# Two value projections as one group of 512 columns, and an earlier broadcast, in a two-layer encoder trunk

## The chip, the cores and the metric

The kernel runs on one core of one Trainium2 chip. The metric is the device time of one launch, in microseconds (us); smaller is better. Five engines work side by side on their own instruction streams: PE (TensorE, matmuls), DVE (VectorE), ACT (ScalarE), POOL (GpSimd) and SP (SyncE, which issues the loads). They meet at semaphores.

## The reference

Two layers, each with four token mixers that read the same normalised input, then gates, an output projection and a gated MLP. Two groups of 256 tokens share all weights; the kernel treats them as 512 tokens. Cut to what matters:

```python
for l in range(DEPTH):                       # DEPTH = 2
    h = rmsnorm(x, attn_norm[l])             # D_MODEL = 1024
    proj = h @ w_in[l]
    a_cols, b_cols, c_cols, d_cols, g_cols = jnp.split(proj, [p1, p2, p3, p4], axis=-1)
    o_a = diff_mixer(a_cols, ...)            # "a": differential attention, values 256 columns
    o_b = natten_mixer(b_cols, b_rpb[l])     # "b": neighbourhood attention with a bias, values 256 columns
    o_c = mla_mixer(c_cols, ...)             # "c": low-rank attention
    o_d = gqa_mixer(d_cols, ...)             # "d": grouped-query attention
    gates = jax.nn.sigmoid(g_cols)
    merged = sum(gates[i] * (o_i @ w_branch[l, i]) for i in range(4))
    x = x + merged @ w_out[l]
    x = x + conv_ffn(rmsnorm(x, ffn_norm[l]), ...)
return rmsnorm(x, final_norm)
```

## The kernel before, in words

**Arithmetic.** Every projection is a product of fp32 data split in two fp32r parts, high and low, and takes three matmuls: high by high, high by low, low by high (`mm3`, L302 to L305; for values L475 to L477). The activations are held as `xh` and `xl`, eight blocks of 128 channels by 512 tokens.

**Pieces.** The weights come as a list of pieces, in a fixed order (`_piece_order`, L133 to L154); a piece is at most 128 partitions by 1280 columns, the ones spoken of here are 128x1024. One piece makes one unit of the main loop (L1241 to L1271). `split_piece` (L284 to L300) makes the high half `wh` of a piece on ACT (L294) and the low half `wl` as a difference, the first half of its columns on DVE (L297) and the rest on POOL (L299). It is called two units ahead (LOOK = 2), and there are three buffers each for raw, high and low pieces, so a piece's high half waits until the matmuls that read the piece three before have ended.

**Order at the start of a layer.** Units are bq0 bk0 bq1 bk1 (queries and keys of the neighbourhood mixer, whose pieces hold two channel blocks of all four, in four PSUM banks), aq0 ak0 (differential mixer), vb0 vb1 (neighbourhood values), aq1 ak1, vd0 vd1 ve0 ve1 vf0 vf1 (the other two mixers), va0 va1 (differential values), then the gates g0 to g31. A value group has two pieces with four channel blocks each. Its first unit issues no matmul, the second issues all 96 with 256 columns: four token tiles, each in a bank of its own over all eight blocks, each copied out by ACT as it ends (`v_unit`, L462 to L479; `v_evac`, L481 to L484).

**Around the change.** The normalisation factor per token, `rs`, is first broadcast to a row by four transposes on PE (`rb`, L364) into the one bank of pool pso; DVE copies it to `rsrow` (`norm_row`, L387 to L403, the copy in L393), and POOL makes `cosr` and `sinr` from it (L400, L401). In layer 0 these transposes are a hook inside aq0, after the third channel block (L602). ak0 uses the same bank of pso. `b_evac` (L636 to L645) scales a bank by `rsrow` on DVE (`bc`, L641), and `split` makes the high half on ACT (L308) and the low half on DVE (L309): bq0h, bq0l, bk0h, bk0l and so on. Scores (`scores_rows`, L784) go to two banks of pool psx; the biased copy `sb` (L795) frees such a bank, then DVE takes the maximum (L801), ACT the exponentials (L807), DVE scales (L817) and PE transposes (L827). `pair_gen` (L851 to L894) spreads these steps over units; PLAG says how many units lie ahead of the product with the values (`po`, L882), CPOS after which gate the first low-rank piece stands. The small `lam` operations (L1232, L1234) are made once. On each engine instructions run in the order in which the program issues them.

Of the kernel before, what the change touches and what calls it, by code (L numbers as in the profile page):

```python
# [32 lines left out]
GX = [(25, 29), (31, 32)]  # L33
GBR = {n: n - BLAG for n in range(BLAG, 30)} | {30: 29, 31: 30}
TLAG = {"a": 1, "b": 1, "c": 0, "d": 0}
PLAG = {"a": 2, "b": 0, "c": 1, "d": 2}
GAP = {"a": 3, "b": 2, "c": 2, "d": 3}
START = {"a": ("ak0", 9), "b": ("bk0", 4), "c": ("cv", 6), "d": ("vf1", 2)}
SLAB = ["bq0", "bk0", "bq1", "bk1"]
CLAG = 1  # L40
CPOS = 7
NEG = -1e30

G_ATTN, G_FFN = 0, 8
# [17 lines left out]
def _col_blocks():  # L62
    r = lambda a, n: list(range(a, a + n))
    blocks = []
    blocks.append(("va", r(A0 + 512, 256)))
    blocks.append(("vb", r(B0 + 512, 256)))
    blocks.append(("vd", r(D0 + 384, 128) + r(D0 + 256, 128)))
    dq = [c for g in range(2) for n in range(2) for c in r(D0 + 128 * n + 64 * g, 64)]
    blocks.append(("ve", r(C0 + 320, 32) + dq))
    blocks.append(("vf", r(C0 + 192, 128) + r(C0, 192)))  # L70
    for j in range(2):
        blocks.append((f"aq{j}", r(A0 + 128 * j, 128)))
        blocks.append((f"ak{j}", r(A0 + 256 + 128 * j, 128)))
    for j in range(2):
        blocks.append((f"bq{j}", r(B0 + 128 * j, 128)))
        blocks.append((f"bk{j}", r(B0 + 256 + 128 * j, 128)))
    return blocks


def _layout_weights(w_in, c_w_uq, c_w_ukv, w_branch, w_out, w_ffn_in, w_ffn_out):  # L80
# [5 lines left out]
    for l in range(DEPTH):  # L86
        p, slab = {}, {}
        for nm, cols in _col_blocks():
            a = kt(w_in[l][:, cols])
            if nm[0] == "v":  # L90
                p[nm + "0"] = a[:, 0:4]
                p[nm + "1"] = a[:, 4:8]
            elif nm in SLAB:
                slab[nm] = a
            else:
                p[nm] = a
        for q, nm in enumerate(SLAB):
            p[nm] = np.stack([slab[b][:, k] for k in (2 * q, 2 * q + 1) for b in SLAB], axis=1)
        z = np.zeros((128, 2, 384), np.float32)
        z[:, 0] = c_w_uq[l][0:128]  # L100
        z[0:64, 1] = c_w_uq[l][128:192]
        p["cq"] = z
        ukv = c_w_ukv[l].reshape(128, 4, 128)
        p["ck"] = ukv[:, :, 0:64]
        p["cv"] = ukv[:, :, 64:128]
        br = []
        for i, d in GSEQ:
            wb = w_branch[l, i]
            if i == 3:
                wb = wb.reshape(2, 2, 64, DM).transpose(1, 0, 2, 3).reshape(256, DM)  # L110
            br.append(kt(wb[:, d * 128:d * 128 + 128]))
        for n, (i, d) in enumerate(GSEQ):
            g = kt(w_in[l][:, G0 + i * DM + d * 128:G0 + i * DM + d * 128 + 128])
            p[f"g{n}"] = np.concatenate([g, br[GBR[n]]], axis=1) if n in GBR else g
        for q, (a, b) in enumerate(GX):
            p[f"gx{q}"] = np.concatenate(br[a:b], axis=1)
        for d in range(ND):
            p[f"wo{d}"] = kt(w_out[l][:, d * 128:d * 128 + 128])
        for j in range(NF):
            p[f"fu{j}"] = kt(w_ffn_in[l][:, j * 128:j * 128 + 128])  # L120
            p[f"fg{j}"] = kt(w_ffn_in[l][:, 2816 + j * 128:2816 + j * 128 + 128])
        fo = kt(w_ffn_out[l])
        for d in range(ND):
            a = fo[:, :, d * 128:d * 128 + 128]
            p[f"fo{d}_0"] = a[:, 0:8]
            p[f"fo{d}_1"] = a[:, 8:15]
            p[f"fo{d}_2"] = a[:, 15:22]
        for nm, a in p.items():
            pieces[(l, nm)] = a
# [3 lines left out]
def _piece_order():  # L133
# [1 line left out]
    two_ = [m for m in ORD if m in "ab"]  # L135
    qk = [[f"{m}q0", f"{m}k0", f"{m}q1", f"{m}k1"] for m in two_]
    assert qk[0] == SLAB
    names += qk[0] + qk[1][:2] + [f"v{two_[0]}0", f"v{two_[0]}1"]
    rest = {"x": qk[1][2:], "w": [f"v{two_[1]}0", f"v{two_[1]}1"], "d": ["vd0", "vd1", "ve0", "ve1"], "c": ["vf0", "vf1"]}
    for ch in 'xdcw':  # L140
        names += rest[ch]
    for n in range(32):
# [65 lines left out]
def trunk_kernel(ctx: ExitStack, tc: tile.TileContext, xt, wflat, gains, lams, rpb, consts, yt):  # L208
# [75 lines left out]
    def split_piece(i, parts=1, only=None):  # L284
# [7 lines left out]
        for q in range(parts):  # L292
            a, b = q * w, q * w + w
            S.activation(out=wh[:, a:b], in_=raw[:, a:b], func=AF.Copy)  # L294
            c = b if only is V else (a + b) // 2
            if c > a:
                V.tensor_tensor(out=wl[:, a:c], in0=raw[:, a:c], in1=f(wh[:, a:c]), op=ALU.subtract)  # L297
            if b > c:
# [26 lines left out]
    st = {}  # L325
# [130 lines left out]
    def build_layer(l):  # L456
# [21 lines left out]
                    evac(t, o)  # L478
            return pe0, pe1  # L479

        def v_evac(vt):  # L481
            def evac(t, o):
                S.activation(out=vt[:, t], in_=o, func=AF.Copy, scale=st["rs"][:, t:t + 1])
            return evac  # L484

        def row_tables():
            def go():
# [105 lines left out]
        def lin(nm, m=128, pool=pm):  # L593
            def pe(wh, wl):
# [4 lines left out]
                w = [a[:, :8 * m].rearrange("p (k c) -> p k c", k=8) for a in (wh, wl)]  # L599
                for k in range(8):  # L600
                    mm3(ps[:m], w[0][:, k], w[1][:, k], st["xh"][k], st["xl"][k], k == 0, k == 7)
                    if k == 2 and pool is pst and "row" in hooks:  # L602
                        hooks.pop("row")()
            return pe

# [494 lines left out]
        specs = {}  # L1100
        for nm in ("aq0", "ak0", "aq1", "ak1"):
            specs[nm] = (lin(nm, pool={"aq0": pst, "ak0": pso}.get(nm, pm)), a_evac(nm))
        for nm, n, ev in (("va", 256, v_evac(vA)), ("vb", 256, v_evac(vB)), ("vd", 256, vd_evac), ("ve", 288, ve_evac),
                          ("vf", 320, vf_evac)):
            pe0, pe1 = v_unit(nm, n, ev)
            specs[nm + "0"], specs[nm + "1"] = (pe0, None), (pe1, None)
# [134 lines left out]
    for i, u in enumerate(units):  # L1241
# [19 lines left out]
        for _, e in now:  # L1261
            e()
        vec(1)
        split_piece(i + LOOK, *((2, V) if i + LOOK < 4 else ()))
        load_piece(i + LOOK + RAW_BUFS)
        if u["now"] and u["evac"] is not None:
            u["evac"]()
# [60 lines left out]
```

## Time and profile before

| what | value |
|---|---|
| median of 3 runs | 1630.31 us (1630.29 to 1631.59) |
| profiled execution: its time | 1630.35 us |
| its span | 1628.6 us |
| PE busy | 1610.0 us, 99% |
| DVE, ACT, POOL busy | 59%, 38%, 40% |
| DMA | 149.26 MB, mean 92 GB/s |

Busy time of PE is from the start of a matmul to its modelled end, and pipelined matmuls overlap; their true pace is the distance between starts. A number in brackets at the end of a row is idle time ahead of the instruction on its engine, with the instruction that released it. "x2" marks instructions in a row that the view has put into one line.

### The profile page before, as it was taken

How to read it: one execution, taken by the hardware profiler on the slowest of the kernel's cores; microseconds unless marked ns; L12 is line 12 of the kernel's file. 1: busy time of each engine (PE TensorE's matmuls, PEld its weight loads, DVE VectorE, ACT ScalarE, POOL GpSimd, SP SyncE). 2: the span in 40 equal slices, each digit the busy share in tenths (PEclk: the TensorE clock that was granted, in tenths of full speed). 3: DMA queues.
4: the chain of work that ended last, by engine and by line, in shares of the span. 5: the costliest groups of instructions: out<-in, count | busy, mean ns of one | idle time of the engine just before them, and what ended most of it. 6: DMA issues, size and time to landing. Idle time of an engine off the chain costs nothing.

```text
span 1628.6 us, 21341 instructions
## 1 busy us (share of the span) xinstructions
PE 1610.0 (99%) x8163; PEld 1336.9 (82%) x8163; DVE 962.7 (59%) x1581; ACT 622.7 (38%) x1112; POOL 653.0 (40%) x443
## 2 busy tenths in 40 slices
PE   9999999999999999999999999999999999999997
PEld 7898788888888888888878977888788888888886
DVE  6767485656775666633366666755468656665113
ACT  4446454332333333322224555434332333333221
POOL 2432223435534444434444231244455344444342
PEclk9999999999999999999999999999999999999998
DMA  7212122221322222232232222222222222222331
GB/s 240 81 53 98 55 98 81 81 78 62 113 91 91 104 104 91 88 105 96 102 115 73 68 89 70 82 87 76 81 78 103 93 97 95 104 91 91 101 97 63
DMA packets 51016, 149.26 MB, mean 92 GB/s; under 512 B 13281, under 2 KB 16353, under 8 KB 50913
## 3 DMA queue, kind: packets, MB, share of 16 engines
q1 hardware_dynamic: 49824, 146.84, 26.5%
q8 instruction: 64, 1.05, 0.2%
q10 hardware_dynamic: 1088, 1.05, 0.2%
q14 instruction: 40, 0.32, 0.1%
HBM read 145.77 MB, written 2.10 MB: 91 GB/s over the span
## 4 chain that ended last, share of the span: by engine, by line
PE 97%; DVE 1%; issue 1%; ACT 1%; POOL 0%; POOLq 0%; DVEq 0%; ACTq 0%
PE pf L303 10%; PE pf L305 10%; PE pf L304 10%; PE pg L303 7%; PE pg L304 7%; PE pg L305 7%; PE pfo L303 5%; PE pfo L305 5%; PE pfo L304 5%; PE po L882 2%; PE pt L827 2%; PE pb L305 2%; PE pwo L304 2%; PE pwo L303 2%; PE pb L303 2%; PE pb L304 2%
## 5 line engine op out<-in xcount | busy, mean ns | idle before, releaser
L299 POOL TENSOR_TENSOR wl<-raw,wh 128x512 fp32r<-128x512 f32 (+4 forms) x258 | 447.3, 1735 | 570.7 <-ACT wh L294 455.3
L294 ACT ACTIVATE wh<-raw 128x1024 fp32r<-128x1024 f32 (+5 forms) x266 | 282.1, 1061 | 437.7 <-PE pfo L304 132.3
L297 DVE TENSOR_TENSOR wl<-raw,wh 128x512 fp32r<-128x512 f32 (+4 forms) x266 | 259.8, 977 | 230.6 <-ACT wh L294 219.2
L303 PE MATMUL pf<-xh,wh 128*128 128x512 f32 x704 | 274.3, 390 | 0.0
L305 PE MATMUL pf<-xh,wl 128*128 128x512 f32 x704 | 274.0, 389 | 0.0
L304 PE MATMUL pf<-xl,wh 128*128 128x512 f32 x704 | 274.0, 389 | 0.0
L303 PE MATMUL pg<-xh,wh 128*128 128x512 f32 x512 | 203.5, 397 | 0.4
L304 PE MATMUL pg<-xl,wh 128*128 128x512 f32 x512 | 199.9, 390 | 0.0
L305 PE MATMUL pg<-xh,wl 128*128 128x512 f32 x512 | 199.6, 390 | 0.0
L305 PEld LDWEIGHTS pf<-xh,wl 128*128 128x128 f32 x704 | 132.1, 188 | 27.7
L304 PEld LDWEIGHTS pf<-xl,wh 128*128 128x128 f32 x704 | 132.2, 188 | 27.3
L303 PEld LDWEIGHTS pf<-xh,wh 128*128 128x128 f32 x704 | 132.2, 188 | 27.1
L303 PE MATMUL pfo<-ah,wh 128*128 128x512 f32 (+1 forms) x374 | 141.1, 377 | 0.0
L304 PE MATMUL pfo<-al,wh 128*128 128x512 f32 (+1 forms) x374 | 140.8, 377 | 0.0
L305 PE MATMUL pfo<-ah,wl 128*128 128x512 f32 (+1 forms) x374 | 140.8, 377 | 0.0
L951 POOL TENSOR_TENSOR mg<-mg,gz 128x512 f32<-128x512 f32 x48 | 64.4, 1346 | 165.5 <-DVE gz L950 165.5
L309 POOL TENSOR_TENSOR al<-fc,ah 128x512 fp32r<-128x512 f32 x44 | 57.8, 1313 | 178.9 <-ACT ah L308 178.9
L303 PEld LDWEIGHTS pg<-xh,wh 128*128 128x128 f32 x512 | 96.2, 188 | 23.4 <-DVE gz L971 1.5
L305 PEld LDWEIGHTS pg<-xh,wl 128*128 128x128 f32 x512 | 96.1, 188 | 20.7
L304 PEld LDWEIGHTS pg<-xl,wh 128*128 128x128 f32 x512 | 96.3, 188 | 18.2
L972 ACT ACTIVATE gz<-gz 128x512 f32<-128x512 f32 x64 | 40.3, 630 | 133.9 <-DVE gz L971 133.8
L807 ACT ACTIVATE pr<-sc,mx 128x256 f32<-128x256 f32 x128 | 59.0, 471 | 73.5 <-DVE mx L802 73.5
(388 smaller groups left out, 2844.6 us busy)
## 6 DMA issues: line engine op xcount, KB each, us to landing
raw<-in_w_dram SPq DMA_DIRECT2D x156, 512.0 KB, 3.2
raw<-in_w_dram SPq DMA_DIRECT2D x58, 640.0 KB, 3.8
raw<-in_w_dram SPq DMA_DIRECT2D x32, 448.0 KB, 3.1
raw<-in_w_dram SPq DMA_DIRECT2D x4, 576.0 KB, 3.4
xall<-in_xt_dram SPq DMA_DIRECT2D x8, 256.0 KB, 5.2
raw<-in_w_dram SPq DMA_DIRECT2D x8, 256.0 KB, 5.3
bias<-in_rpb_dram SPq DMA_DIRECT2D x32, 64.0 KB, 3.3
out_dram<-y SPq DMA_DIRECT2D x4, 256.0 KB, 2.4
```

The source lines that it names most:

```text
L294: S.activation(out=wh[:, a:b], in_=raw[:, a:b], func=AF.Copy)
L297: V.tensor_tensor(out=wl[:, a:c], in0=raw[:, a:c], in1=f(wh[:, a:c]), op=ALU.subtract)
L299: G.tensor_tensor(out=wl[:, c:b], in0=raw[:, c:b], in1=f(wh[:, c:b]), op=ALU.subtract)
L303: PE.matmul(ps, lhsT=wh, rhs=xh, start=first, stop=False)
L304: PE.matmul(ps, lhsT=wh, rhs=xl, start=False, stop=False)
L305: PE.matmul(ps, lhsT=wl, rhs=xh, start=False, stop=last)
L309: (eng or V).tensor_tensor(out=l, in0=v, in1=f(h), op=ALU.subtract)
L807: S.activation(out=p[:, qt * 256:qt * 256 + 256], in_=src[c][:, qt * 256:qt * 256 + 256], func=AF.Exp, scale=sc, bias=mx[:, i:i + 1], accu ...
L827: PE.transpose(out=ps[:, kt * 256 + qt * 128:kt * 256 + qt * 128 + 128], in_=p[:, qt * 256 + kt * 128:qt * 256 + kt * 128 + 128], identity ...
L882: PE.matmul(ops[64 * e:64 * e + 64, :256], lhsT=v_of(mix, j, e, 2 * b + kt), rhs=pt[:, kt * 256:kt * 256 + 256], start=(kt == 0), stop=(kt ...
L951: G.tensor_tensor(out=m, in0=m, in1=z, op=ALU.add)
L972: S.activation(out=z, in_=z, func=AF.Tanh, scale=0.5)
```

## The change

The two groups of 256 value columns become one group "vw" of 512 columns, neighbourhood first. Its four pieces hold two channel blocks each, and stand where vb0 and vb1 stood: vw0 to vw3, then aq1, ak1, vd, ve, vf, gates. All four token tiles are open at once, in four banks, and the channel blocks are the outer loop over the pieces; within the last piece the token tile is the outer loop, so that the banks end one after another. ACT makes its eight copies of 256 columns after vw3. The broadcast hook in aq0 comes after the first channel block. In layer 0 the low halves of pieces 6 and 7 (vw0 and vw1, before vb0 and vb1) are made by POOL alone, in one instruction each. PLAG of the neighbourhood mixer is 4, and CPOS is 9.

```diff
-PLAG = {"a": 2, "b": 0, "c": 1, "d": 2}
+PLAG = {"a": 2, "b": 4, "c": 1, "d": 2}
...
-CPOS = 7
+CPOS = 9
...
-    blocks.append(("va", r(A0 + 512, 256)))
-    blocks.append(("vb", r(B0 + 512, 256)))
+    blocks.append(("vw", r(B0 + 512, 256) + r(A0 + 512, 256)))
...
+            if nm == "vw":
+                for q in range(4):
+                    p[f"vw{q}"] = a[:, 2 * q:2 * q + 2]
...
-    names += qk[0] + qk[1][:2] + [f"v{two_[0]}0", f"v{two_[0]}1"]
-    rest = {"x": qk[1][2:], "w": [f"v{two_[1]}0", f"v{two_[1]}1"], "d": ["vd0", "vd1", "ve0", "ve1"], "c": ["vf0", "vf1"]}
+    names += qk[0] + qk[1][:2] + [f"vw{q}" for q in range(4)]
+    rest = {"x": qk[1][2:], "w": [], "d": ["vd0", "vd1", "ve0", "ve1"], "c": ["vf0", "vf1"]}
...
-            c = b if only is V else (a + b) // 2
+            c = b if only is V else a if only is G else (a + b) // 2
...
+        def vw_pe(q):
+            def pe(wh, wl):
+                if q == 0:
+                    D["vw"] = [psum("psvw") for _ in range(4)]
+                w = [a[:, :1024].rearrange("p (k c) -> p k c", k=2) for a in (wh, wl)]
+                kt = [(k, t) for k in range(2) for t in range(4)]
+                if q == 3:
+                    kt.sort(key=lambda i: i[1])
+                for k, t in kt:
+                    d = 2 * q + k
+                    xh = st["xh"][d][:, t * 128:t * 128 + 128]
+                    xl = st["xl"][d][:, t * 128:t * 128 + 128]
+                    o = D["vw"][t]
+                    PE.matmul(o, lhsT=xh, rhs=w[0][:, k], start=(d == 0), stop=False)
+                    PE.matmul(o, lhsT=xh, rhs=w[1][:, k], start=False, stop=False)
+                    PE.matmul(o, lhsT=xl, rhs=w[0][:, k], start=False, stop=(d == 7))
+            return pe
+
+        def vw_evac():
+            for t, o in enumerate(D.pop("vw")):
+                for vt, c in ((vB, 0), (vA, 256)):
+                    S.activation(out=vt[:, t], in_=o[:, c:c + 256], func=AF.Copy, scale=st["rs"][:, t:t + 1])
...
-                    if k == 2 and pool is pst and "row" in hooks:
+                    if k == 0 and pool is pst and "row" in hooks:
...
+        for q in range(4):
+            specs[f"vw{q}"] = (vw_pe(q), vw_evac if q == 3 else None)
...
-        split_piece(i + LOOK, *((2, V) if i + LOOK < 4 else ()))
+        split_piece(i + LOOK, *((2, V) if i + LOOK < 4 else (1, G) if i + LOOK in (6, 7) else ()))
```

DVE in layer 0, from the row factor on, before (`rs2` is its square, `wl6` and `wl7` are low halves of pieces 6 and 7, `lam` the lambda values):

```order
L397 TENSOR_TENSOR rs2_406<-rs_332 128x4
L297 TENSOR_TENSOR wl6_456<-raw6_265,wh6_455 128x512
L1232 TENSOR_TENSOR lam_85<-lp_346 128x1 x2
L1234 TENSOR_SCALAR lam_85<-lam_85 128x1 x2
L297 TENSOR_TENSOR wl7_524<-raw7_296,wh7_523 128x512
L393 COPY rsrow_404<-rb_399 128x512
L641 TENSOR_TENSOR bc_427<-psbq0_199,rsrow_404 128x8x64
L309 TENSOR_TENSOR bq0l_430<-bc_427,bq0h_429 128x512
```

The same place now:

```order
L399 TENSOR_TENSOR rs2_400<-rs_332 128x4
L1254 TENSOR_TENSOR lam_85<-lp_346 128x1 x2
L1256 TENSOR_SCALAR lam_85<-lam_85 128x1 x2
L395 COPY rsrow_398<-rb_393 128x512
L661 TENSOR_TENSOR bc_427<-psbq0_199,rsrow_398 128x8x64
L311 TENSOR_TENSOR bq0l_430<-bc_427,bq0h_429 128x512
```

The two low halves are gone from DVE, and the copy of the broadcast row follows the lambda values directly; POOL's instructions on wl6 and wl7 are 128x1024 in the same places of its own order.

DVE further on in layer 0, between the scalings of the first softmax and the biased copy of the second, before:

```order
L630 TENSOR_TENSOR rc_513<-rc_513,rsh_514 128x512
L810 RECIPROCAL ri_503<-su_502 128x2
L817 TENSOR_SCALAR sb_504<-sb_504,ri_503 128x256 x2
L309 TENSOR_TENSOR aq0l_520<-rc_513,aq0h_519 128x512
L795 SCALAR_TENSOR_TENSOR sb_533<-sc_463,bias1_374 128x512
```

The same place now:

```order
L650 TENSOR_TENSOR rc_512<-rc_512,rsh_513 128x512
L830 RECIPROCAL ri_502<-su_501 128x2
L837 TENSOR_SCALAR sb_503<-sb_503,ri_502 128x256 x2
L299 TENSOR_TENSOR wl9_641<-raw9_459,wh9_640 128x512
L311 TENSOR_TENSOR aq0l_519<-rc_512,aq0h_518 128x512
L815 SCALAR_TENSOR_TENSOR sb_559<-sc_462,bias1_374 128x512
```

A low half, that of piece 9, now stands ahead of the biased copy that frees the second score bank.

PE where the values of layer 0 meet the second pair of scores (`psvb` and `psvw` are banks of the values, `sc` of scores), before:

```order
L477 MATMUL psvb_573<-wh7_523,xl7_184 128x256
L475 MATMUL psvb_599<-wh6_455,xh0_123 128x256
L784 MATMUL sc_559<-bk0h_435,bq0h_429 128x256
L784 MATMUL sc_559<-bk0l_436,bq0h_429 128x256
L784 MATMUL sc_559<-bk0h_435,bq0l_430 128x256
```

The same place now:

```order
L496 MATMUL psvw_531<-wh6_455,xh1_140 128x512
L497 MATMUL psvw_531<-wl6_456,xh1_140 128x512
L498 MATMUL psvw_531<-wh6_455,xl1_141 128x512
L804 MATMUL sc_585<-bk0h_435,bq0h_429 128x256
L804 MATMUL sc_585<-bk0l_436,bq0h_429 128x256
```

The scores stood behind 25 matmuls of 256 columns, the last of them of the second token tile; now they stand behind the 24 of vw0, with 512 columns. The next six scores, of the other bank, stood 37 matmuls of 256 columns later, and stand 13 of 512 later now.

## Rows read from the trace of the kernel before

**Rows 1.** Page, parts 1 and 4: busy us by engine; the chain's shares by engine.
```profile
PE 1610.0 (99%) x8163; PEld 1336.9 (82%) x8163; DVE 962.7 (59%) x1581; ACT 622.7 (38%) x1112; POOL 653.0 (40%) x443
...
PE 97%; DVE 1%; issue 1%; ACT 1%; POOL 0%; POOLq 0%; DVEq 0%; ACTq 0%
```

**Rows 2.** Waits of PE: us in total, times, longest.
```profile
PE sc L784 <- DVE sb L795: 2.6, 3, 1.1
...
PE psak L303 <- DVE rsrow L393: 2.4, 1, 2.4
```

**Rows 3.** Timeline of PE, values: start, us, line, tile, shape; first and last of 95.
```profile
123.89 0.28 PE L476 MATMUL psva<-wl,xh 128*128 128x256 f32 x1
...
135.16 0.28 PE L477 MATMUL psva<-wh,xl 128*128 128x256 f32 x1
```

**Rows 4.** Timeline of PE, matmuls of 512 columns, first and last of 24.
```profile
19.84 0.39 PE L303 MATMUL psbq<-xh,wh 128*128 128x512 f32 x1
...
25.06 0.39 PE L305 MATMUL psbk<-xh,wl 128*128 128x512 f32 x1
```

**Rows 5.** Timeline of PE in layer 0, from aq0's last matmul to the values.
```profile
34.64 0.39 PE L305 MATMUL psaq<-xh,wl 128*128 128x512 f32 x1
37.41 0.47 PE L303 MATMUL psak<-xh,wh 128*128 128x512 f32 x1 [2.39 <-DVE rsrow L393]
...
42.60 0.39 PE L784 MATMUL sc<-bk0l,bq0h 64*128 64x256 f32 x2
...
44.66 0.28 PE L475 MATMUL psvb<-wh,xh 128*128 128x256 f32 x1
...
48.90 0.35 PE L784 MATMUL sc<-bk0h,bq0h 64*128 64x256 f32 x1 [1.10 <-DVE sb L795]
...
54.93 0.35 PE L784 MATMUL sc<-bk0h,bq0h 64*128 64x256 f32 x1 [0.58 <-DVE sb L795]
...
55.80 0.39 PE L476 MATMUL psvb<-wl,xh 128*128 128x256 f32 x1
```

**Rows 6.** Timeline of DVE in layer 0.
```profile
30.63 1.31 DVE L1232 TENSOR_TENSOR lam<-lp 128x1 f32<-128x1 f32 x2
...
35.97 0.69 DVE L297 TENSOR_TENSOR wl<-raw,wh 128x512 fp32r<-128x512 f32 x1 [3.85 <-ACT wh L294]
36.58 0.68 DVE L393 COPY rsrow<-rb 128x512 f32<-128x512 f32 x1
...
40.90 1.65 DVE L309 TENSOR_TENSOR bk0l<-bc,bk0h 128x512 fp32r<-128x512 f32 x1 [0.70 <-ACT bk0h L308]
...
46.38 1.78 DVE L309 TENSOR_TENSOR bk1l<-bc,bk1h 128x512 fp32r<-128x512 f32 x1
48.08 0.68 DVE L795 SCALAR_TENSOR_TENSOR sb<-sc,bias 128x512 f32<-128x512 f32 x1
...
54.10 0.68 DVE L795 SCALAR_TENSOR_TENSOR sb<-sc,bias 128x512 f32<-128x512 f32 x1
```

**Rows 7.** Timeline of ACT in layer 0: piece 7's high half, a copy of values.
```profile
34.88 1.06 ACT L294 ACTIVATE wh<-raw 128x1024 fp32r<-128x1024 f32 x1 [4.80 <-POOL bias L744]
...
47.73 0.47 ACT L483 ACTIVATE vB<-psvb,rs 128x256 f32<-128x256 f32 x1 [1.48 <-PE psvb L477]
```

**Rows 8.** Timeline of POOL in layer 0: piece 6's low half, sinr.
```profile
30.07 1.79 POOL L299 TENSOR_TENSOR wl<-raw,wh 128x512 fp32r<-128x512 f32 x1 [5.00 <-ACT wh L294]
...
39.01 1.75 POOL L401 TENSOR_TENSOR sinr<-rsrow,cst 128x512 f32<-128x512 f32 x1
```

**Rows 9.** Groups of POOL by form: busy us, mean ns of one, idle before.
```profile
L497 POOL TENSOR_TENSOR rt<-cst,lv 128x256 f32<-128x256 f32 x8 | 5.9, 737 | 0.0
...
L400 POOL TENSOR_TENSOR cosr<-rsrow,cst 128x512 f32<-128x512 f32 x2 | 2.6, 1293 | 0.0
```

**Rows 10.** Timelines of PE and DVE in layer 1, second score bank.
```profile
849.91 0.38 PE L784 MATMUL sc<-bk0h,bq0h 64*128 64x256 f32 x1 [0.92 <-DVE sb L795]
...
849.17 0.68 DVE L795 SCALAR_TENSOR_TENSOR sb<-sc,bias 128x512 f32<-128x512 f32 x1
```

More of the change, by code (lines that the diff above doesn't have):

```diff
@@ L89, in _layout_weights @@
             a = kt(w_in[l][:, cols])
-            if nm[0] == "v":
+            if nm == "vw":
+                for q in range(4):
+                    p[f"vw{q}"] = a[:, 2 * q:2 * q + 2]
+            elif nm[0] == "v":
                 p[nm + "0"] = a[:, 0:4]
@@ L479, in v_unit @@
             return pe0, pe1
[L481 to L484, printed above, removed]
+        def vw_pe(q):
[19 more added lines that the diff above has]
+                    S.activation(out=vt[:, t], in_=o[:, c:c + 256], func=AF.Copy, scale=st["rs"][:, t:t + 1])
         def row_tables():
@@ L1102, in build_layer @@
             specs[nm] = (lin(nm, pool={"aq0": pst, "ak0": pso}.get(nm, pm)), a_evac(nm))
-        for nm, n, ev in (("va", 256, v_evac(vA)), ("vb", 256, v_evac(vB)), ("vd", 256, vd_evac), ("ve", 288, ve_evac),
+        for q in range(4):
+            specs[f"vw{q}"] = (vw_pe(q), vw_evac if q == 3 else None)
+        for nm, n, ev in (("vd", 256, vd_evac), ("ve", 288, ve_evac),
                           ("vf", 320, vf_evac)):
```

## The prediction

> **What bounds the kernel now.** I read the page's busy shares and its chain first, then the table of TensorE's waits, then the timeline where those waits stand. TensorE is busy 99% of the span and is 97% of the chain [rows 1]. A change can therefore gain in two ways only: fewer or shorter matmuls, or the removal of one of the few places where TensorE stands still. Those places are known: it waits for the row factor's copy once, 2.4 us, and for a score bank three times, 2.6 us in all [rows 2]. The profiled execution took 1630.35 us, 0.04 above the median of 1630.31; my sum is made against 1630.35, of which the span is 1628.6. All of the span counts, since TensorE fills it to its end.
>
> **Packing.** Removed: 192 matmuls of 256 columns per layer (two groups of four token tiles, eight blocks, three terms). Added: 96 of 512 columns. With 256 columns, 95 matmuls in a row start between 123.89 and 135.16, 94 steps of 0.1199 us [rows 3]. With 512 columns, 24 in a row start between 19.84 and 25.06, 23 steps of 0.2270 [rows 4]. Two small ones cost 0.2398, one large one 0.2270: 0.0128 saved per pair, 96 pairs per layer, two layers: **2.46 us**. The Trainium skill ("TensorE: Matmul & The Clock Gate", Back-to-back issue gap) gives a matmul its columns at 2.4 GHz and 2.5 ns; by that the packing would save 192 × 2.5 ns = 0.5 us. The rows show five times that per matmul and decide, since both forms stand in this trace with the same operand type. Bounds: nothing (if the new matmuls run at 0.2398, as the order of their operands is new) and 2.5.
>
> **The hook, and the splits moved to POOL (layer 0 only).** Before, aq0's last matmul starts at 34.64, so ak0 could start near 34.87; it starts at 37.41 [rows 5], because ak0 takes the bank of the broadcast, and DVE copies that bank only at 36.58, behind the low split of piece 7, which waits for ACT's high half [rows 6, 7]. Now the broadcast stands six matmuls earlier (some 1.36 us, so near 29.6) and DVE has no split of pieces 6 and 7. What then blocks the copy is less: the two tiny lambda operations stood from 30.63 to 31.94 while POOL did its half of piece 6 [rows 6, 8]. That half becomes a whole: 128x256 takes 0.737 on POOL and 128x512 1.293 [rows 9], so 0.556 for 256 more, and 128x1024 is an estimate of 1.293 + 2 × 0.556 = 2.4. POOL starts at 30.07, so lambda runs at 32.45 and the copy ends near 33.3. ak0 follows aq0 without a wait: **2.54 us earlier**.
>
> Little of it is kept. ACT's order is unchanged: the high half of piece 7, held until aq0 gives its buffer back, runs from 34.88 to 35.94 [rows 7], and only then bq0's high half, to 36.5. POOL's low split of piece 7 starts then too and lasts to about 38.4. DVE's low half of bq0 needs two inputs from SBUF, as POOL does. Such DVE instructions take 0.69 alone and 1.65 or 1.78 beside a POOL instruction [rows 6], ending about 0.55 after it: they wait for it to finish. The rows show this for POOL instructions of 1.3 us, none for one of 2.4. The Trainium skill ("SBUF — State Buffer", Who interferes with whom) has the shared pair as a lock held for the whole instruction, which speaks against handing POOL whole splits; if it holds, bq0's low half ends at 38.9, if the pair is given up half way, near 37.2. I take the first, as the nearest rows do the same. Then follow bk0's copy (39.5), 0.7 for its high half (the idle time ahead of its low half in [rows 6], 40.2), and its low half, behind sinr, which POOL takes first (1.75 in [rows 8], 1.3 without a rival): it ends near 41.9. Before, it ended at 42.55 and the first scores that read it started at 42.60 [rows 5, 6]. So TensorE, 2.5 us ahead, waits some 2 us more there, and is **0.67 us ahead** when the values start: 43.99, not 44.66.
>
> Before, the second pair of scores comes one by one: the first after 25 small matmuls, where TensorE stands still about 1.25 us until 48.90, the second another 0.75 until 54.93 (by start steps; the idle times of the rows are 1.10 and 0.58) [rows 5]. Now they stand behind 24 and 37 large ones. TensorE reaches the first at 43.99 + 24 × 0.227 = 49.44, when DVE's biased copy for them, started at 48.08 before and 0.6 earlier now, is done: no wait. It reaches the second at 53.26. Their bank is freed by DVE's next biased copy, which was at 54.10 [rows 6]. That copy now has the split of piece 9 ahead of it, since vw0's buffer comes back after 24 matmuls and not after a whole group. Piece 9's high half runs to 52.15, POOL holds its low half to 53.45 (1.3), DVE's scalings (0.6), own half (0.69) and aq0's low half (0.69) follow it: the copy ends near 55.8, and **the wait is 2.5 instead of 0.75**. Were POOL no obstacle there, 1.9.
>
> Set side by side at the restart: before at 55.80 with 130 small matmuls left (15.6 us, ends 71.4); now, after six score matmuls, at 56.7 with 59 large ones left (13.4 us, ends 70.1). **Layer 0 gains 1.33 us**: 1.23 is packing, so the removed waits (2.54, 1.25, 0.75) come back as waits of about 2 and 2.5 almost in full.
>
> **Layer 1** has neither hook nor the POOL splits; there the order alone changes. Its second scores started at 849.91 after an idle 0.92 (1.14 by start steps), because the bank was freed by a copy from 849.17 on [rows 10]. They now stand behind vw0, 5.4 us later, and the wait goes: **1.14**, with 1.23 of packing. The split that now gets ahead of the next biased copy does not delay TensorE: that copy stands before it there.
>
> **What costs nothing.** Eight ACT copies of 256 columns per layer, as before, 0.47 each [rows 7], but now in one go after vw3. aq1 takes the first bank alone, which is complete 18 matmuls (4.1 us) before the group ends, while ACT needs 0.94 for its two copies and about as much for the exponentials between. Were that cover gone, each layer would wait up to all eight. Four banks for the group: the last needs bk1's scaled copy, at 44.5, and is first written at 46.0. vw0 and vw1 need POOL's whole splits by 44 and 49.5; they are done at 32.5 and 38.4. PLAG 4 puts neighbourhood's products later, when their values exist; CPOS 9 moves the low-rank projections two gates later, and the three score waits of [rows 2] all lie ahead of the gates [rows 5, 10]. Loads have the same sizes and count.
>
> **Sum:** 1.33 + 1.14 + 1.23 = 3.70 to take from 1630.35, **1626.65 us**. About 0.2% (3.26 us, so 1627.05 and below) is what a measurement of this kernel can tell from no change; the forecast is just past it.
>
> **Rivals.**
> *A, packing alone.* Each wait removed, layer 1's too, comes back elsewhere. For it: layer 0 does so by my working. Against it: no instruction stands newly ahead of layer 1's copy. 1630.35 − 2.46 = 1627.9, no measurable change.
> *B, the waits of layer 0 go for good.* If POOL does not hold DVE during the long splits (or they are shorter than 2.4), bq0's and bk0's low halves end near 37.2 and 39.3, TensorE hardly waits for the first scores, and the chain behind follows 2.5 us earlier: 2.54 + 0.15 + 1.25 + 0.75 = 4.7 saved, with 2.46 and 1.14 it is 8.3: 1622.0; half of it is 1624.5. For it: the chain bk0, biased copy, scaling is all that is late. Against it: 1.65 and 1.78 in [rows 6].
> *C, the packing doesn't pay.* The new matmuls load token tiles as weights and step at 0.2398, not 0.2270; then 2.46 falls away and 1629.1 is left, no change. Against it: weight loads are as large in [rows 4]. The skill's 2.5 ns, by itself, would leave 1628.6, in the same class.
> *D, slower.* One group holds all four banks, and its copies come at the end. If ACT is held by the exponentials between (they wait for DVE's maxima), and the first bank's two copies finish more than 4.1 us after its last matmul, aq1 waits, and ak1 after it; with all eight, 8 × 0.47 = 3.75 per layer, or 7.5 in two. 1626.65 + 7.5 = 1634.15. It decides between vw3's end and aq1's first matmul. For it: an exponential and a copy of transposes stand ahead of them in ACT's order, and both wait on other engines. Against it: what these wait for is done before vw3 begins.
>
> **Numbers.** Forecast 0.49 (its own range 1625.6 to 1627.6, by 1 us either way for the two waits of layer 0 that I worked out), A 0.20, B 0.17, C 0.06, D 0.08. Faster: B's 0.17 and some 0.39 of the forecast, 0.56. Same: A, C and the forecast's upper tenth, 0.36. Slower: D, 0.08. The range runs from half of B's gain past the forecast, 1623.8, to between A and C, 1628.6; D, the far half of B and part of C are left out, about 2 in 10.
>
> **What would show it.** Right: value matmuls at steps of 0.227; ak0 less than 0.3 after aq0; TensorE idle about 2 us at the first scores for bk0's low half; POOL's 128x1024 near 2.4 and DVE's bq0 low half near 2.4 beside it; no wait at the second scores in either layer; one of about 2.5 at the next, behind the split of piece 9. Wrong: an idle TensorE ahead of aq1 or ak1 (D), a step of 0.24 (C), DVE at 0.69 beside POOL's long split (B), or waits in the gates of either layer, where none is now.

## The result, and the profile after

The change makes the kernel slower: 1651.43 us (median of 4, 1649.76 to 1653.64) against 1630.9, a ratio of 1.0122 with a 95% interval of 1.0109 to 1.0134. The prediction was 1626.65, the range 1623.8 to 1628.6. The profiled execution took 1649.76 us, its span 1648.0, that is 19.4 us more than the span of before.

TensorE is hardly busier than before (1613.8 us against 1610.0), but the chain now lies 91% on it, where it was 97% [rows 1]. The rest is waits; first the chain's shares, then lines of the table of TensorE's waits of the changed kernel (us in total, times, longest):

```profile
PE 91%; DVE 4%; issue 2%; ACT 2%; POOL 0%; SPq 0%; DMA 0%; POOLq 0%; ACTq 0%; DVEq 0%
```

```profile
PE pg L305 <- DVE cql L311: 6.1, 2, 3.1
PE pg L305 <- DVE gz L991: 4.8, 2, 2.4
...
PE po L902 <- ACT ptr L853: 2.4, 2, 1.2
PE sc L804 <- DVE sb L815: 2.2, 1, 2.2
PE psve L477 <- DVE rtm L534: 1.5, 2, 0.8
...
PE sc L804 <- ACT bk0h L310: 1.4, 1, 1.4
PE cv L738 <- DVE cql L311: 1.4, 2, 0.7
...
PE sc L804 <- DVE bk0l L311: 0.6, 1, 0.6
```

Those that stand twice, once per layer, are all new and all lie behind the place that the prediction worked out: among the projections (psve), the gates (pg), and the low-rank pieces (cv). Before, TensorE had no wait there: beside the lines of [rows 2] its table has only waits at the ends of the kernel and at each layer's broadcast. The single ones are the layer-0 waits that were forecast.

**Layer 0, up to the values: as forecast.** TensorE's timeline of the changed kernel (start, us, line, tile, idle time ahead), answering to [rows 5]:

```profile
35.21 0.39 PE L305 MATMUL psak<-xh,wh 128*128 128x512 f32 x1
...
40.63 0.38 PE L804 MATMUL sc<-bk0h,bq0h 64*128 64x256 f32 x2 [1.41 <-ACT bk0h L310]
...
42.27 0.39 PE L804 MATMUL sc<-bk0l,bq0h 64*128 64x256 f32 x2 [0.60 <-DVE bk0l L311]
...
44.33 0.39 PE L496 MATMUL psvw<-wh,xh 128*128 128x512 f32 x1
...
49.86 0.38 PE L804 MATMUL sc<-bk0h,bq0h 64*128 64x256 f32 x1
...
56.23 0.35 PE L804 MATMUL sc<-bk0h,bq0h 64*128 64x256 f32 x1 [2.23 <-DVE sb L815]
```

ak0 follows aq0 without a wait, 2.0 us are then lost at the first scores, the second pair's first scores don't wait, its second wait 2.2. DVE and POOL (a timeline, and POOL's group of that form) show why:

```profile
30.46 2.44 DVE L1254 TENSOR_TENSOR lam<-lp 128x1 f32<-128x1 f32 x2 [0.87 <-ACT lp L1251]
...
33.00 0.68 DVE L395 COPY rsrow<-rb 128x512 f32<-128x512 f32 x1
...
36.84 2.47 DVE L311 TENSOR_TENSOR bq0l<-bc,bq0h 128x512 fp32r<-128x512 f32 x1 [2.44 <-ACT bq0h L310]
...
55.40 0.68 DVE L815 SCALAR_TENSOR_TENSOR sb<-sc,bias 128x512 f32<-128x512 f32 x1
```

```profile
L301 POOL TENSOR_TENSOR wl<-raw,wh 128x1024 fp32r<-128x1024 f32 x2 | 4.8, 2398 | 5.7 <-ACT wh L296 5.7
```

A low half that takes 0.69 us alone [rows 6] takes 2.47 beside POOL's instruction of 2.40.

**The gates: where the time went.** TensorE, DVE and POOL in layer 0 (the same in layer 1):

```profile
156.98 0.65 PE L902 MATMUL po<-ptr,vA 128*64 128x256 f32 x4 [1.20 <-ACT ptr L853]
160.04 0.50 PE L305 MATMUL pg<-xh,wh 128*128 128x512 f32 x1 [2.42 <-DVE gz L991]
...
241.39 0.48 PE L305 MATMUL pg<-xh,wh 128*128 128x512 f32 x1 [3.06 <-DVE cql L311]
```

```profile
149.89 1.97 DVE L579 TENSOR_TENSOR dr<-dr,r 128x384 f32<-128x384 f32 x4
151.77 1.28 DVE L821 TENSOR_REDUCE mx<-sc 128x2 f32<-128x512 f32 x2
...
156.64 2.15 DVE L839 SCALAR_TENSOR_TENSOR pr<-pr,ri 128x256 f32<-128x256 f32 x2
158.72 0.68 DVE L821 TENSOR_REDUCE mx<-sc 128x2 f32<-128x512 f32 x1
159.32 0.67 DVE L991 TENSOR_TENSOR gz<-pg,rsrow 128x512 f32<-128x512 f32 x1
...
236.93 1.53 DVE L321 TENSOR_TENSOR nt<-nt,nh 128x16 f32<-128x16 f32 x1
238.50 0.17 DVE L322 SCALAR_TENSOR_TENSOR ny<-nt,ny 128x16 f32<-128x16 f32 x1
238.71 0.76 DVE L669 COPY ex<-ny 128x512 f32<-128x512 f32 x2
...
240.57 0.68 DVE L311 TENSOR_TENSOR cql<-tq,cqh 96x512 fp32r<-96x512 f32 x1
```

```profile
236.24 2.19 POOL L301 TENSOR_TENSOR wl<-raw,wh 128x640 fp32r<-128x640 f32 x1 [3.87 <-ACT wh L296]
```

DVE in the same place of layer 0 before:

```profile
150.93 1.28 DVE L801 TENSOR_REDUCE mx<-sc 128x2 f32<-128x512 f32 x2
...
155.79 0.88 DVE L819 SCALAR_TENSOR_TENSOR pr<-pr,ri 128x256 f32<-128x256 f32 x2
```

At 160 the gate waits for a bank that DVE's `gz` frees, and DVE comes to it only after the differential pair's scalings, held by a split on POOL (2.15 us for two that took 0.88 in the same place before). That hold is 1.3 us. The rest began earlier: the pair's maxima start 4.4 us after its scores (151.77 after 147.37), 1.4 before the change (150.93 after 149.53); ahead of them on DVE now stand the late normalisation's steps, the four `dr` last. The exponentials follow the maxima, and behind them and a piece's high half on ACT stands the copy `ptr` (from 156.32), for which the products wait at 157.

At 241 the gate waits for `cql`. Ahead of that on DVE stand the last Newton steps (the iteration for the reciprocal square root) and copies of the differential mixer's normalisation, and one of these steps took 1.53 us instead of 0.17, beside POOL's half of the next piece. What a wait costs does not end with it. The windows of the changed kernel (length, TensorE busy, granted clock, DMA share, GB/s):

```profile
156.00:160.00 4.00, 0.65 (x4) 1.00 0.00 0
160.00:165.00 5.00, 4.96 (x15) 0.66 0.41 131
...
970.00:976.00 6.00, 5.71 (x18) 0.72 0.32 109
...
1050.00:1056.00 6.00, 4.45 (x13) 0.72 0.24 96
```

After TensorE stood nearly still from 156 to 160, the granted clock fell from 2.4 to 1.2 GHz for about 3 us (0.66 over 5 us; large matmuls start 0.43 apart instead of 0.227), which costs (1 − 0.66) × 5 = 1.7 us more. The other two windows give 0.28 × 6 = 1.7 each.

By start steps (the distance between two starts, less the step that the matmuls ahead had among themselves), the new waits are 0.93 (psve), 1.51 and 2.67 (157 and 160), 3.28 (241) and 0.87 (cv) per layer, 9.26, so 18.5 in two layers. With three slow stretches of 1.7 that is 23.6. Less the 3.70 that the prediction had as gain, 19.9 is left; the spans differ by 19.4. The idle times in the rows are 0.2 to 0.3 shorter each; with them it would be 17.6.

### The profile page after: what moved, and what is told of

Same layout as the page of the kernel before. It is cut to its first block, busy times and chain, and to the rows that moved or that the text cites. A ratio compares the mean times of both kernels' runs of the same rounds, so it can differ in the third digit from the quotient of the medians.

```text
span 1648.0 us, 20960 instructions
## 1 busy us (share of the span) xinstructions
PE 1613.8 (98%) x7971; PEld 1329.3 (81%) x7971; DVE 952.8 (58%) x1579; ACT 621.6 (38%) x1112; POOL 657.6 (40%) x443
## 4 chain that ended last, share of the span: by engine, by line
PE 91%; DVE 4%; issue 2%; ACT 2%; POOL 0%; SPq 0%; DMA 0%; POOLq 0%; ACTq 0%; DVEq 0%
PE pf L305 10%; PE pf L306 10%; PE pf L307 10%; PE pg L305 7%; PE pg L306 7%; PE pg L307 7%; PE pfo L305 5%; PE pfo L307 5%; PE pfo L306 5%; PE po L902 2%; PE pwo L306 2%; PE pwo L305 2%; PE pwo L307 2%; PE pb L306 2%; PE pb L305 2%; PE pb L307 2%
## 5 line engine op out<-in xcount | busy, mean ns | idle before, releaser
L301 POOL TENSOR_TENSOR wl<-raw,wh 128x512 fp32r<-128x512 f32 (+5 forms) x258 | 450.7, 1747 | 576.1 <-ACT wh L296 499.2
L299 DVE TENSOR_TENSOR wl<-raw,wh 128x512 fp32r<-128x512 f32 (+4 forms) x264 | 251.2, 951 | 239.4 <-ACT wh L296 227.1
L991 DVE TENSOR_TENSOR gz<-pg,rsrow 128x512 f32<-128x512 f32 x64 | 43.9, 686 | 70.5 <-PE pg L307 70.4
```

The costliest lines, as they stand in the source:

```text
L301: G.tensor_tensor(out=wl[:, c:b], in0=raw[:, c:b], in1=f(wh[:, c:b]), op=ALU.subtract)
L991: V.tensor_tensor(out=z, in0=pg, in1=st["row"], op=ALU.mult)
```

## The experiments

All times are medians; each ratio is to the kernel before, run beside it (1631.65 to 1631.93 us in these runs).

**What part of the change makes the loss.** Four kernels, each the kernel before with a part of it. The first has the new order of the pieces, with PLAG and CPOS as in the change, but two value groups of 256 columns.

```diff
-PLAG = {"a": 2, "b": 0, "c": 1, "d": 2}
+PLAG = {"a": 2, "b": 4, "c": 1, "d": 2}
...
-CPOS = 7
+CPOS = 9
...
-    for ch in 'xdcw':
+    for ch in 'wxdc':
```

> The kernel before with the order of the pieces changed alone: both value groups stay apart, of 256 columns each, but the differential values stand right behind the neighbourhood's, and the other two mixers' projections come two units later; PLAG of the neighbourhood mixer is 4 and CPOS 9 as in the change. No packing, hook and splits as before. Phase theory (the change's loss is that the normalisation of the other two mixers and the three low-rank pieces now fall into the same units as the softmax steps of the differential and grouped-query pairs): about 1650 us, with TensorE waits near 157, 160, 241 and 251 us as in the change. Packing theory (four banks held at once and k outermost make the loss): within 2 us of 1630. Layer-0 theory (hook and POOL splits delay all that follows): within 2 us of 1630.

Measured: 1659.26, ratio 1.0170 (1.0155 to 1.0185), with every one of the new waits: 0.91 before psve, 1.50 and 2.68 near 160, 3.28 and 0.87 near 244 and 255. So the order with CPOS, without packing, makes more than the whole loss.

```diff
-CPOS = 7
+CPOS = 9
```

> The kernel before with CPOS 9 instead of 7 alone: the low-rank pieces two gates later, everything else where it was. If the low-rank units alone cause the waits at 241 and 251 us (3.28 and 0.87 us, in both layers) it is some 8 us slower, about 1638; the waits at 157 and 160 are absent. If it takes both (normalisation late and pieces late), it is within 2 us of 1630.

Measured: 1647.84, ratio 1.0093 (1.0077 to 1.0110). The two waits are there at their size (3.28 and 0.87) and none near 157. They make 8.3 us; the forecast of 8 had left out the clock, which in the profiled execution was low in four stretches of 1.7 each:

```profile
36.00:42.00 6.00, 4.41 (x13) 0.72 0.59 204
...
236.00:242.00 6.00, 3.37 (x8) 0.72 0.32 111
...
858.00:864.00 6.00, 5.40 (x32) 0.72 0.27 87
...
1050.00:1056.00 6.00, 6.00 (x21) 0.72 0.00 0
```

The first and the third stand behind ak0's wait of 2.4 us and behind the 1.1 us wait of [rows 10], which this kernel has as the kernel before has them; in that one's profiled execution the clock stayed at 1.00 behind both.

```diff
-PLAG = {"a": 2, "b": 0, "c": 1, "d": 2}
+PLAG = {"a": 2, "b": 4, "c": 1, "d": 2}
```

> The kernel before with PLAG of the neighbourhood mixer 4 instead of 0 alone: its products with the values four units later. Phase theory: within 2 us of 1630, as these are 8 short matmuls per pair beside gates. Rival (the later products take the pso bank and ACT's copies when the differential pairs want them): slower by 5 to 20 us, with a wait of TensorE near 157 us.

Measured: 1632.14, ratio 1.0000 (0.9991 to 1.0009). PLAG costs nothing that can be measured.

```diff
-                    if k == 2 and pool is pst and "row" in hooks:
+                    if k == 0 and pool is pst and "row" in hooks:
...
-            c = b if only is V else (a + b) // 2
+            c = b if only is V else a if only is G else (a + b) // 2
...
-        split_piece(i + LOOK, *((2, V) if i + LOOK < 4 else ()))
+        split_piece(i + LOOK, *((2, V) if i + LOOK < 4 else (1, G) if i + LOOK in (6, 7) else ()))
```

> The kernel before with the broadcast after the first channel block and the low halves of pieces 6 and 7 wholly on POOL, nothing else. By the prediction's working ak0 follows aq0 without a wait (2.5 us), TensorE then waits some 2 us for the low half of bk0, and of the gain 0.7 us is left when the values start; the waits at the second scores are 0.6 shorter or the same: 1629 to 1630.5. If POOL's long instructions don't hold DVE: 1626 to 1628. Layer-0 theory: over 1640.

Measured: 1630.10, ratio 0.9992 (0.9983 to 1.0001): ak0 2.5 us earlier, 2.0 us of it lost again at the first scores (1.41 and 0.60 by the waits, as in the changed kernel), the later score waits nearly as before (idle 1.20 and 0.57). The values start 9.35 us after aq0's last matmul, where it was 10.02 before: the 0.67 of the prediction. Its working holds up to there.

**Why the low-rank pieces wait.** In the kernel before with CPOS 9, and in the changed kernel, the Newton steps were to move out of unit ck, by two more pauses ahead of them and two fewer behind:

```diff
             V.tensor_scalar(out=ms, in0=ps[:, :16], scalar1=1.0 / 64, scalar2=EPS, op0=ALU.mult, op1=ALU.add)
+            yield
+            yield
             y = newton(ms, 16)
...
             yield
-            yield
-            yield
             for j in range(2):
                 pb = psum("ab", pso)
```

> The kernel before with CPOS 9, and the Newton steps of the differential mixer's normalisation (16 small DVE operations and two copies) issued one unit later, out of the short unit ck; the normalisation ends where it did. Collision theory (DVE's Newton steps, one of them held by POOL's split, stand ahead of the low half of cq, whose bank the next gate waits for): the wait of 3.28 us before the gate behind ck goes in both layers, and with it TensorE's slower clock after it: some 10 us less than CPOS alone, near 1637. Rival (the low-rank unit ck is too short wherever it stands between these softmax steps): near 1648.

> The changed kernel with the same move of the Newton steps out of unit ck. Collision theory: the wait at 241 us of the changed kernel goes in both layers, those at 157 and 160 stay: near 1641. Rival: near 1651.

Measured: 1647.74 (ratio 1.0096, 1.0081 to 1.0111) and 1654.44 (1.0139, 1.0124 to 1.0154). Neither expectation: the wait of 3.28 shrank to 1.92, but the transposes that need the Newton result, now close behind it, wait in turn. TensorE in the first of the two:

```profile
237.38 0.47 PE L303 MATMUL pg<-xh,wh 128*128 128x512 f32 x1 [1.71 <-DVE cql L309]
...
248.01 0.63 PE L364 MATMUL ab<-cst,ex 128*128 128x128 f32 x4 [3.15 <-DVE ex L649]
```

The edit moved less than was meant. The built program does not keep the source's order among these DVE steps: the first of them (L313, at 234.76) still stood ahead of `cql`, the next (L314) came at 243.50. And the first was the one that POOL held now (POOL and DVE in the first of the two kernels):

```profile
233.81 2.19 POOL L299 TENSOR_TENSOR wl<-raw,wh 128x640 fp32r<-128x640 f32 x1 [3.87 <-ACT wh L294]
```

```profile
234.76 1.28 DVE L313 TENSOR_SCALAR ny<-am 128x16 int32<-128x16 int32 x1
```

A third try put the differential pairs one unit earlier, so that Newton falls beside a gate (the new lag of "d" keeps the grouped-query pairs, which follow them, in their old units):

```diff
-START = {"a": ("ak0", 9), "b": ("bk0", 4), "c": ("cv", 6), "d": ("vf1", 2)}
+START = {"a": ("ak0", 8), "b": ("bk0", 4), "c": ("cv", 6), "d": ("vf1", 11)}
...
-CPOS = 7
+CPOS = 9
```

> The kernel before with CPOS 9 and the differential pairs one unit earlier (START of a at ak0 + 8), so that the whole Newton sequence of their normalisation, up to the two copies, falls beside a gate and not in unit ck; the grouped-query pairs stay in their units. Collision theory: no wait of 3 us at the gate behind ck, nor its slow clock; CPOS then costs 2 us or less there, apart from new waits that the earlier pairs may meet near 140 to 170. Rival (ck too short in itself): the wait at 238 stays above 2 us.

Measured: 1658.54, ratio 1.0161 (1.0146 to 1.0176). The wait fell to 1.71 by start steps, less than the rival asked for and more than the theory allowed. New ones came at cv (2.28 and 0.98 twice, for cq's low halves and ACT's copies), a little ahead of it (1.3 idle) and near 154 (0.6). With Newton gone, POOL's split (233.14 to 235.33) held the scalings that now stood in the place (0.61 for these two elsewhere):

```profile
234.21 1.54 DVE L817 TENSOR_SCALAR pr<-pr,ri 128x256 f32<-128x256 f32 x2
```

So Newton's place makes 1.4 to 1.6 of the 3.28. In all these kernels POOL's half of the next piece holds a DVE instruction close behind DVE's own half: it takes 1.4 us longer than alone in the changed kernel, 1.1 where L313 is the one, 0.9 with the scalings. Taken off, about 0.8 is left of 1.92 and of 1.71, for the grouped-query pair's DVE work in a short unit (six large matmuls in ck, twelve small ones in cv). This is an estimate from these rows: no run took that split from POOL or cut it in two. What would take all of the wait away was not found.

**The normalisation's share.** CPOS back to 7 in the changed kernel needs an earlier start or a shorter pause of the other mixers' normalisation.

```diff
-CLAG = 1
+CLAG = 0
-CPOS = 9
+CPOS = 7
```

> The changed kernel with CPOS 7, so that the low-rank pieces stand where they stood before; to have their inputs in time the transposes of the other two mixers begin without the pause of two steps (CLAG 0), so they too fall where they did before, while the normalisation ahead of them stays two units later. If CPOS 9 is 16 us of the loss: no waits at 241 and 251, 1636 or less. If the waits at 157 and 160 come from the later transposes they go too and it is near 1627; if from the later normalisation (ACT's scalings ahead of the exponentials) they stay, near 1636.

```diff
-        at(pos["vf1"] + 1, cd_gen)
+        at(pos["vf1"], cd_gen)
...
-CPOS = 9
+CPOS = 7
```

> The changed kernel with CPOS 7 and the normalisation of the other two mixers begun one unit earlier, right behind their last projection: one unit later than before the change instead of two, transposes too. No waits at 241 and 251. If the collision with the differential pairs (every third unit) is what makes the waits at 157 and 160, one unit instead of two moves them or takes them away: between 1626 and 1636.

Measured: 1639.97 (1.0049, 1.0033 to 1.0066), with waits of 1.90 for the normalised input of the transposes and 0.8 to 0.9 idle at psve; and 1634.37 (1.0014, 1.0005 to 1.0024), with 0.94 at psve and one wait of 2.23 per layer for the gate. In both the waits at 241 and 251 are gone; the times are 11.5 and 17.1 us below the changed kernel's. The same question from the other side, normalisation two units later in the kernel before:

```diff
-        at(pos["vf1"] + 1, cd_gen)
+        at(pos["vf1"] + 3, cd_gen)
...
-CPOS = 7
+CPOS = 9
```

> The kernel before with CPOS 9 and the normalisation of the other two mixers begun two units later, while all projections and value groups stay where they were: only the phase of normalisation and low-rank pieces against the softmax steps is that of the change. If this phase alone makes the loss: the waits at 157 and 160 appear as well, about 10 us more than CPOS alone, near 1657, and none at 110 (that one belongs to the later projections). If the waits at 157 and 160 need the later projections too: near 1648.

Measured: 1652.36, ratio 1.0127 (1.0111 to 1.0142), between the two expectations: 4.5 more than CPOS alone. One wait of 2.40 per layer near 160 (where the changed kernel has 2.67), none at 157 and none at 110; those two need the later projections.

**Is the packed group itself free?** First with aq1 and ak1 behind the other projections, so that these end in their old unit:

```diff
-CPOS = 9
+CPOS = 7
...
-    for ch in 'xdcw':
+    for ch in 'dcxw':
```

> The changed kernel with the second query and key pieces of the differential mixer (aq1, ak1) behind the projections of the other two mixers instead of ahead of them, and CPOS 7. So these projections end in the same unit as before the change, and normalisation, low-rank pieces and all softmax steps from there on stand to each other as before; packing, four banks, hook, POOL splits and PLAG are those of the change. Phase theory: all waits from 105 us on that the change has and the kernel before has not are gone, and what is left is the prediction's sum: 1626 to 1628. Packing theory (four banks and k outermost cost something of their own): above 1632.

The second has, beyond that, hook and splits as before the change; the third is the first with piece 7 in two halves:

> The same as the realigned one, with the hook behind the third channel block and the low halves of pieces 6 and 7 half on DVE and half on POOL, as before the change. By the prediction's working hook and splits give the values 0.67 us and nearly all of it goes at the second score bank: within 1 us of the realigned kernel, with ak0 late by 2.5 us, the first scores without a wait.

```diff
-        split_piece(i + LOOK, *((2, V) if i + LOOK < 4 else (1, G) if i + LOOK in (6, 7) else ()))
+        split_piece(i + LOOK, *((2, V) if i + LOOK < 4 else (1, G) if i + LOOK == 6 else (2, G) if i + LOOK == 7 else ()))
```

> The realigned kernel with POOL making the low half of piece 7 as two instructions of 512 columns instead of one of 1024. If POOL holds DVE for a whole instruction, DVE's low half of bq0 waits for the first of them only, the chain to the first scores is about 1 us shorter, and TensorE's wait of 2.3 us there shrinks to about 1.2: 0.5 to 1 us faster than the realigned kernel. If not, the same within 0.5.

Measured: 1642.40 (1.0062, 1.0045 to 1.0078), 1644.28 (1.0078, 1.0063 to 1.0093) and 1641.45 (1.0056, 1.0041 to 1.0071). The waits of the change are gone, but DVE's rotation of ak1 has come into the units of the normalisation, and the transposes wait for it:

```profile
PE tr L596 <- DVE rsh L648: 5.2, 2, 2.6
...
PE pg L305 <- DVE gz L991: 2.2, 2, 1.1
```

That is a miss for what was asked; and the first two are 1.9 us apart, where 1 was forecast. The third kernel answers another question well, the hold of POOL on DVE:

```profile
36.69 0.85 DVE L311 TENSOR_TENSOR bq0l<-bc,bq0h 128x512 fp32r<-128x512 f32 x1 [2.53 <-ACT bq0h L310]
```

```profile
55.11 0.55 PE L804 MATMUL sc<-bk0h,bq0h 64*128 64x256 f32 x1 [2.86 <-DVE sb L815]
```

With two instructions of 512 columns in place of one of 1024, DVE's low half takes 0.85 instead of 2.47: it gets in between. The first scores that read bk0l came 5.79 us after aq0's last matmul, 7.29 in the first kernel: 1.5 shorter, more than the 1 expected, and the wait at the second bank grew from 2.23 to 2.86; the two kernels' times can't be told apart.

Then the group was made of other columns, so that nothing behind it moves: neighbourhood values with the grouped-query mixer's values and keys, while the differential values stay apart, last (the tables for the rotation of vd are made in vw2).

```diff
-    blocks.append(("vw", r(B0 + 512, 256) + r(A0 + 512, 256)))
-    blocks.append(("vd", r(D0 + 384, 128) + r(D0 + 256, 128)))
+    blocks.append(("vw", r(B0 + 512, 256) + r(D0 + 384, 128) + r(D0 + 256, 128)))
+    blocks.append(("va", r(A0 + 512, 256)))
...
-CPOS = 9
+CPOS = 7
...
-    rest = {"x": qk[1][2:], "w": [], "d": ["vd0", "vd1", "ve0", "ve1"], "c": ["vf0", "vf1"]}
+    rest = {"x": qk[1][2:], "w": ["va0", "va1"], "d": ["ve0", "ve1"], "c": ["vf0", "vf1"]}
...
-                for vt, c in ((vB, 0), (vA, 256)):
-                    S.activation(out=vt[:, t], in_=o[:, c:c + 256], func=AF.Copy, scale=st["rs"][:, t:t + 1])
+                S.activation(out=vB[:, t], in_=o[:, :256], func=AF.Copy, scale=st["rs"][:, t:t + 1])
+                vd_evac(t, o[:, 256:512])
...
```

> The changed kernel, but the group of 512 columns is made of the neighbourhood's values and the grouped-query mixer's values and keys (vd); the differential values stay a group of 256 columns behind the other projections, as before the change, and CPOS is 7. So ve, vf, va, the normalisation, the low-rank pieces and all softmax steps from there on stand in their old units; packing (96 large matmuls for 192 small ones in each layer), four banks, k outermost, hook, POOL splits and PLAG 4 are as in the change. Phase theory: the waits behind 105 us go, and what remains is the prediction's sum, 1626 to 1628; a new wait of up to 2 us per layer is possible ahead of aq1, since the first bank now comes free only after DVE's rotation of vd. Packing theory (held banks or k outermost cost by themselves): 1632 or more, with waits inside the group or right behind it.

> The same with hook and splits as before the change. Prediction's working: ak0 2.5 us later, first scores 2.3 us less wait, nearly the same end: within 1 us of the run with hook and splits.

Measured: **1629.34**, ratio 0.9985 (0.9975 to 0.9994, 10 runs), faster than both kernels, by 1.0 to 4.1 us than the kernel before; and 1631.53, ratio 0.9997 (0.9988 to 1.0007), not to be told from the kernel before. In the first, TensorE's waits, beside those at the ends of the kernel and at each layer's broadcast, which the kernel before has too, are the ones that the prediction worked out:

```profile
PE sc L807 <- DVE sb L818: 2.2, 1, 2.2
...
PE sc L807 <- ACT bk0h L310: 1.4, 1, 1.4
...
PE sc L807 <- DVE bk0l L311: 0.6, 1, 0.6
PE psva L477 <- ACT pr L830: 0.3, 2, 0.2
```

Four banks held and the contraction outermost cost nothing. Layer 1, which has neither hook nor POOL splits, shows packing by itself, from its broadcast to the sums at the end (kernel before, then the first of the two):

```profile
824.62 0.62 PE L364 MATMUL rb<-cst,rs 128*128 128x128 f32 x4 [0.76 <-DVE rs L359]
...
1617.60 0.61 PE L421 MATMUL stf<-cst,sqf 128*128 128x1 f32 x4 [0.97 <-DVE sqf L417]
```

```profile
826.49 0.62 PE L366 MATMUL rb<-cst,rs 128*128 128x128 f32 x4 [0.82 <-DVE rs L361]
...
1617.32 0.61 PE L423 MATMUL stf<-cst,sqf 128*128 128x1 f32 x4 [0.97 <-DVE sqf L419]
```

That is 792.98 us before and 790.83 now, and 790.86 in the kernel without hook and splits: 2.15 and 2.12 less, where the prediction has 1.14 and 1.23, 2.37. No slow clock stands in these stretches. The gain of the whole kernel is 2.6 us instead of 3.7; in its profiled execution the clock fell to 0.60 and 0.55 in the two windows of 2 us behind the 2.2 us wait of layer 0, which is (0.40 + 0.45) × 2 = 1.7.

The second kernel is 2.2 us behind the first, where 1 was forecast: a miss. In its profiled execution the clock was 0.72 over 6 us behind ak0's wait and 0.66 over 10 behind the second score bank's, 1.7 and 3.4 us. So what packing is worth in layer 0 can't be read from its time.

## Why the prediction was wrong

**Packing, right.** 183 steps within the group have a median of 0.227 us, as taken from [rows 4]; rival C is out. With the same packed form and nothing moved behind it, layer 1 is 2.1 us shorter with hook and splits or without, and the kernel with both is 2.6 us faster.

**Hook and splits, right in mechanism and size.** ak0 without a wait; POOL's 128x1024 2.398 us (estimate 2.4); DVE's low half held for the whole instruction, 2.47 (2.4 forecast); two waits of 2.0 together at the first scores (some 2 forecast); no wait at the next; then 2.23, or 2.39 by start steps (2.5 forecast). The run with two instructions in place of one shows the same from the other side. The Trainium skill's lock for the whole instruction ("SBUF — State Buffer", Who interferes with whom) agrees with both. Rival B is out. What hook and splits gain in the kernel's time (0.1 by the sum) is too little to be measured.

**Layer 1, right.** The wait of 1.14 is gone.

**What failed is the paragraph "What costs nothing", in its sentence on CPOS**: "CPOS 9 moves the low-rank projections two gates later, and the three score waits of [rows 2] all lie ahead of the gates". That TensorE waits nowhere among the gates before says nothing about units that are moved against the DVE and ACT work of the pairs. CPOS alone measured +16 us: 8.3 are the new waits and 3.4, in the one trace, the slow clock behind them; for the other 4 no cause is shown (two more slow stretches there stand behind waits that the kernel before has too). Not costed at all was the second move that the change contains: vd, ve, vf and the normalisation behind them come two units later, while the pairs' steps stay in their units; later normalisation measured 4.5 us on top of CPOS (the 2.40 near 160), and the waits at 110 and 157 come with the later projections. The shares don't add up exactly: the order with CPOS gave 27 us, and the slow clock behind the same waits differs from trace to trace.

Rival D had the sign, and the wrong mechanism: aq1 and ak1 follow the group without a wait in the changed kernel. The gates were named among the things that would prove the forecast wrong ("waits in the gates of either layer, where none is now"), but no rival was made of it, so its chance was nil. One bound of its range is a slip: half of B's gain past the forecast comes to 1624.3, not 1623.8; nothing hangs on it. The step to have taken is the one taken for layer 0: the order of DVE and ACT in each unit from vf1 to cv, before and after, with durations from the rows.

Still open are the 0.8 us estimated for the low-rank wait without POOL's hold, and whether a placement of the original group of values exists in which nothing collides; the nearest one tried had a ratio of 1.0014 to the kernel before.

## What to carry to other kernels

When work is inserted ahead of a pipeline of staged steps, everything behind it shifts against the steps that do not shift, and a place without a wait is no proof that another alignment has none: list, for each unit that moves, what stands ahead on every engine's queue in its new neighbourhood. Pack what leaves the rest in its place; here packing other columns turned a loss of 20 us into a gain of 2.6 (1.0 to 4.1). Price a new wait with the slow clock that may follow it, here mostly 1.7 us on top of a wait of 1.1 to 3.3, at most 3.4 behind a single place.

## What the runs showed of the hardware

The slow clock behind a wait is not settled by the wait's length. Behind waits of 2.67 it came in both layers (0.66 over 5 us, 0.72 over 6); behind the 3.28 it came in layer 1 of the changed kernel and not in layer 0; behind a wait of 1.1 us it came with CPOS alone and not in the kernel before; behind the 2.2 us wait of layer 0 it came in the fastest kernel and not in the changed one. Behind ak0's wait of 2.4 us it came with CPOS alone and not in the kernel before, which are the same program up to there. Where waits followed closely it lasted: with the pairs one unit earlier, 0.57 over the 12 us from 250, 5.2 us. The times of one kernel spread too (the kernel before took 1629.92 to 1634.21 in 13 runs); that the clock makes this spread is likely, but not shown.

A tiny DVE operation can be held by POOL as a large one: one Newton step of 128x16 elements took 1.53 us instead of 0.17 beside POOL's split of a piece, and the two lambda operations 2.44 us beside the one of 1024 columns.
